# Expert weights in transfers of 2 MB, in the places of the attention's tiles, and gate's last steps behind the gather

## The chip, the cores and the metric

The kernel runs on one core of a Trainium2 chip. The metric is device time of one execution, in microseconds: the median of three timed runs. Profiles are of one execution, which has its own time.

## What is computed

The whole network of three blocks, on 256 tokens of width 1024 in float32. The first block is attention (a windowed unit with grouped heads, and a latent unit) and a mixture of 16 experts. The second is an S5 mixer and a feed-forward block, the third a "fox" attention and a feed-forward block; both are modulated by shift, scale and gate vectors from `silu(c) @ ada_w`. A final norm ends it. The part that the change touches most:

```python
def expert_choice_ffn(h, w_router, w_gate, w_up, w_down):
    cap = CAPACITY_FACTOR * seq // N_EXPERTS      # 2 * 256 // 16 = 32
    aff = softmax(einsum('bsd,de->bse', h, w_router))
    gate, idx = lax.top_k(aff.transpose(0, 2, 1), cap)
    xe = vmap(lambda hb, ib: hb[ib])(h, idx)
    a = silu(einsum('becd,edf->becf', xe, w_gate)) * einsum('becd,edf->becf', xe, w_up)
    ye = einsum('becf,efd->becd', a, w_down) * gate[..., None]
    y = zeros((seq, d)).at[idx].add(ye)           # for each batch
```

Each of w_gate, w_up and w_down is 16 x 1024 x 1024 in float32; together they are 192 tiles of 1 MB, and each is used once.

## The kernel before

Weights come from HBM in the order of one list (`plan` appends to it). `fill` issues the next loads of the list on SP's queue as long as there is a slot; SP then waits, in order, until each slot's last reader is done. A slot is 8 KB in each of the 128 partitions (128x2048 floats, 1 MB), and the pool `big` has 22 of them (NSLOT). Weights share it with the attention's tiles (xT, cn, cT, rev, qk, bqk, qTbv, pT, bqT) and later ones. `weights(room, look, hires, cap)` sets how many slots `fill` leaves free in a stage; `KN` holds these numbers by stage. `done` gives a slot back and calls `fill`.

The experts go in four groups g of four. In a group, for each half hf of the inner width, eight steps k multiply a tile of w_gate and a tile of w_up (four experts side by side on the PE array, into PSUM tiles `pg` and `pu`); after that 16 tiles of w_down give `py`, two halves of eight, each followed by a scatter (`scat`) that adds to h through a one-hot matrix. Tables of the S5 mixer (the `filler`) are computed among the products from the end of the second group on.

Ahead of the experts stands the route (`moe_route`): the affinities' transposes `affT`, eight top-8 steps on DVE, `bi` (indices spread on a diagonal) and the matmul `pidx` that gives them to all partitions, one-hot matrices `oh`, and the gather, eight steps of two matmuls `xe`, interleaved with the first group's first half. Between top-8 and `bi`, `pump(8)` works off the last gate matmuls of the side list: `gate_step` multiplies a piece of `ada_w` with silu(c), and at its last piece copies the sum (`gr`), transposes it, adds a bias (`gc`), transposes again and writes it as a row to DRAM (`row_out`); `fetch` reads it back, near the end of the experts.

Ada loads are eight pieces of 1 MB of `ada_w` for each norm; `ada` are their matmuls, which stand wherever the list of loads brings them. The S5 mixer has four groups n: `u(n)` (a product with a w_in tile), `S` (the chunk's states), a scan with `re`/`im` transposes, `y` and `glu`. `s5m` is the number of loads at the end of the experts' list that stand behind S5's first w_in load.

## Time and profile before

| | us |
|---|---|
| median of three timed runs (1296.58 to 1298.2) | 1297.32 |
| the profiled execution | 1299.42 |
| span of its trace | 1297.1 |
| PE busy | 1109.0 (85%) |
| DVE busy | 658.7 (51%) |
| ACT busy | 401.4 (31%) |
| POOL busy | 107.0 (8%) |

DMA moves 379.35 MB, 292 GB/s in the mean. PE, DVE, ACT and POOL are the four engines, SP the one that issues most DMAs. In the rows below a timeline's line gives start, duration, engine, line of the code, operation, tiles (out<-in), shapes, count, and in brackets the idle time before it with what ended it. The mean granted clock of PE was 0.909.

### The profile page before, as it was taken

The numbers are of one execution on the slowest core, as the hardware profiler recorded it, in microseconds if no ns is written. First come the engines' busy times: TensorE is split into PE (matmuls) and PEld (weight loads), VectorE is DVE, ScalarE is ACT, GpSimd is POOL, SyncE is SP. The second block draws the span as 40 slices with busy tenths as digits, with TensorE's granted clock in tenths as the row PEclk, the third lists the DMA queues.
The fourth block names the chain that finished last, engine by engine and source line by source line (L and its number), as shares of the span: only waits on it lengthen the run. The fifth ranks groups of instructions, "written<-read, shape, count | busy, mean of one in ns | idle before, by whom it ended". The sixth has DMA issues, their size and how long they took to land.

```text
span 1297.1 us, 19439 instructions
## 1 busy us (share of the span) xinstructions
PE 1109.0 (85%) x7775; PEld 747.0 (58%) x7775; DVE 658.7 (51%) x1523; ACT 401.4 (31%) x841; POOL 107.0 (8%) x117
## 2 busy tenths in 40 slices
PE   8989898566666776665989999999999989999997
PEld 7654431011021511100757889998879776999986
DVE  5663401028079507002467666764557765667652
ACT  6352110000000100001014274643444652655541
POOL 2111000010000000000131300000010013200001
PEclk9999897767787867676989999999999989999999
DMA  8994699999999999999775544639665765437420
GB/s 336 389 416 153 260 367 419 418 420 419 420 420 419 418 420 418 420 419 419 308 295 194 194 172 171 247 144 360 209 234 190 289 252 223 142 141 271 153 108 33
DMA packets 61382, 379.35 MB, mean 292 GB/s; under 512 B 6723, under 2 KB 8499, under 8 KB 19692
## 3 DMA queue, kind: packets, MB, share of 16 engines
q1 hardware_dynamic: 60364, 374.49, 73.0%
q0 software_dynamic: 496, 3.23, 0.6%
q8 instruction: 61, 1.00, 0.3%
q10 hardware_dynamic: 432, 0.40, 0.1%
q14 instruction: 29, 0.24, 0.0%
HBM read 376.96 MB, written 1.13 MB: 291 GB/s over the span
## 4 chain that ended last, share of the span: by engine, by line
PE 57%; DMA 29%; DVE 7%; issue 4%; ACT 1%; POOL 1%; SPq 0%; POOLq 0%; DVEq 0%; ACTq 0%
PE up L359 20%; DMA w<-in_w_down_dram 11%; PE acc L359 11%; DMA w<-in_w_up_dram 9%; DMA w<-in_w_gate_dram 6%; PE qk L359 3%; PE wo L359 2%; PE glu L359 2%; PE v L359 2%; DMA row<-row_dram 2%; PE zl L359 1%; PE zq L359 1%; PE xe L359 1%; PE po L359 1%; PE ada L359 1%
## 5 line engine op out<-in xcount | busy, mean ns | idle before, releaser
L291 DVE TENSOR_TENSOR wlo<-w,whi 128x512 fp32r<-128x512 f32 (+4 forms) x284 | 215.8, 821 | 50.3 <-ACT whi L291 46.1
L291 ACT CAST whi<-w 128x512 fp32r<-128x512 f32 (+4 forms) x304 | 191.6, 705 | 69.8 <-PE acc L359 25.8
L359 PE MATMUL up<-xTh,whi 128*128 128x256 f32 x704 | 199.9, 285 | 0.9 <-ACT whi L291 0.9
L359 PE MATMUL up<-xTl,whi 128*128 128x256 f32 x704 | 199.3, 284 | 0.2 <-DVE xTl L400 0.2
L359 PE MATMUL up<-xTh,wlo 128*128 128x256 f32 x704 | 198.8, 283 | 0.0
L359 PEld LDWEIGHTS up<-xTh,whi 128*128 128x128 f32 x704 | 135.4, 193 | 4.9 <-ACT cv L1690 1.7
L359 PEld LDWEIGHTS up<-xTl,whi 128*128 128x128 f32 x704 | 135.3, 192 | 0.6 <-DVE xTl L400 0.6
L359 PE MATMUL py<-w,aT 128*32 128x512 f32 x512 | 91.7, 806 | 51.2 <-DMA w<-in_w_down_dram 51.1
L359 PEld LDWEIGHTS up<-xTh,wlo 128*128 128x128 f32 x704 | 135.1, 192 | 0.2 <-DVE wlo L291 0.2
L359 PE MATMUL pg<-w,xe 128*32 128x512 f32 x512 | 87.6, 761 | 33.4 <-DMA w<-in_w_gate_dram 33.4
L359 PE MATMUL pu<-w,xe 128*32 128x512 f32 x512 | 85.8, 744 | 34.5 <-DMA w<-in_w_up_dram 34.5
L359 PEld LDWEIGHTS py<-w,aT 128*32 128x32 f32 x512 | 12.2, 124 | 119.0 <-DMA w<-in_w_down_dram 102.4
L359 PE MATMUL acc<-whi,gTh 128*128 128x512 f32 (+1 forms) x220 | 76.5, 348 | 0.0
L359 PE MATMUL acc<-whi,gTl 128*128 128x512 f32 (+1 forms) x220 | 76.4, 347 | 0.0
L359 PE MATMUL acc<-wlo,gTh 128*128 128x512 f32 (+1 forms) x220 | 76.2, 347 | 0.0
L402 DVE SCALAR_TENSOR_TENSOR yl<-py,gcol,yh 128x512 fp32r<-128x512 f32 x8 | 6.0, 751 | 127.0 <-ACT yh L401 127.0
L359 PEld LDWEIGHTS pu<-w,xe 128*32 128x32 f32 x512 | 13.9, 120 | 93.3 <-DMA w<-in_w_up_dram 79.0
L359 PEld LDWEIGHTS pg<-w,xe 128*32 128x32 f32 x512 | 13.0, 120 | 89.0 <-DMA w<-in_w_gate_dram 76.4
L1222 DVE TENSOR_TENSOR a<-pu,a 128x512 f32<-128x512 f32 x8 | 5.5, 691 | 107.3 <-PE pu L359 107.3
L401 ACT ACTIVATE yh<-py,gcol 128x512 fp32r<-128x512 f32 x8 | 5.5, 687 | 152.9 <-PE py L359 152.9
L1691 DVE SCALAR_TENSOR_TENSOR cv<-up,small,cv 128x255 f32<-128x255 f32 x44 | 20.9, 482 | 52.9 <-ACT cv L1690 52.7
L1221 ACT ACTIVATE a<-pg 128x512 f32<-128x512 f32 x8 | 4.8, 597 | 136.6 <-PE pg L359 136.6
(451 smaller groups left out, 2001.7 us busy)
## 6 DMA issues: line engine op xcount, KB each, us to landing
w<-in_w_gate_dram SPq DMA_DIRECT2D x64, 1024.0 KB, 19.9
w<-in_w_up_dram SPq DMA_DIRECT2D x64, 1024.0 KB, 19.9
w<-in_w_down_dram SPq DMA_DIRECT2D x64, 1024.0 KB, 19.9
w<-in_ada_t_dram SPq DMA_DIRECT2D x48, 1024.0 KB, 11.3
w<-in_ffn_w_up_dram SPq DMA_DIRECT2D x44, 1024.0 KB, 5.5
w<-in_ffn_w_down_dram SPq DMA_DIRECT2D x22, 1024.0 KB, 7.5
w<-in_fox_w_in_dram SPq DMA_DIRECT2D x12, 1024.0 KB, 5.5
row<-row_dram SPq DMA_DIRECT2D x24, 256.0 KB, 6.8
```

The lines of the kernel that those rows point to most:

```text
L291: for ins in (hc(hi[:, f], t[:, f]), e.tensor_tensor(lo[:, f], t[:, f], hi[:, f].bitcast(F32), op=OP.subtract)):
L359: r = self.nc.tensor.matmul(out, lhsT, rhs, start=start, stop=stop)
L401: return (nc.scalar.mul(dst.hi, src, a), nc.vector.scalar_tensor_tensor(dst.lo, src, a, dst.hi.bitcast(F32), op0=OP.mult, op1=OP.subtract))
L402: nc.vector.scalar_tensor_tensor(dst.lo, src, a, dst.hi.bitcast(F32), op0=OP.mult, op1=OP.subtract))
L1221: nc.scalar.activation(a, pg, AF.Silu)
L1222: nc.vector.tensor_tensor(a, pu, a, op=OP.mult)
L1691: v.scalar_tensor_tensor(cv[:, 1:], a[:, :T - 1], cw[1], cv[:, 1:], op0=OP.mult, op1=OP.add)
```

## The change

Two expert tiles become one transfer. On the host `w_gu` lays w_gate and w_up of a step side by side, `w_dn` two steps of w_down; such a double is 128x4096, 16 KB in each partition, 2 MB. Only the first group's odd steps stay single (`ones`): 24 transfers of 1 MB and 84 of 2 MB in place of 192 of 1 MB.

The slots are split. `big` keeps 14 single ones. Two pools at either side, "l" and "r", have four single slots each, which hold the attention's tiles (xT, rev and bqk left; xt, cn, cT, qk, qTbv, pT and bqT right); when these tiles have been read for the last time, `place` turns each pool into two double ones, and after the experts into four single ones again. So there are at most four doubles at a time. `free` takes tiles, not a count, and `can` asks the pool that a load would go to.

In the route, `held` keeps gate's last steps (`gate_end`) until behind the gather, `one` is made ahead of the top-8 steps, and gather and first half are held in program order. Two numbers of the order change: `s5m` from 4 to 2 (still 4 MB), and `w_moe1`.

```diff
@@ -24,6 +24,8 @@
 NSLOT = 22
+TWOS = 2
-      "sd_firstf": "", "L1": 6, "foxL": 2, "hip": 1, "rm1": -1, "w_moe1": [2, 1, 6],
+      "sd_firstf": "", "L1": 6, "foxL": 2, "hip": 1, "rm1": -1, "w_moe1": [0, 1, 0],
...
-      "s5m": 4, "sd_fox": "a11 g10", "w_ffn01": [7, 2, 2],
+      "s5m": 2, "sd_fox": "a11 g10", "w_ffn01": [7, 2, 2],
+def ones(g, name, hf, k):
+    return (g == 0 or g == 1 and name == "gu" and hf < 0) and k % 2 > 0
-    for name in ("w_gate", "w_up", "w_down"):
-        o[name] = i[name].reshape(4, 4, 8, 128, 2, 512).transpose(0, 4, 2, 3, 1, 5)
+    w = {name: i[name].reshape(4, 4, 8, 128, 2, 512).transpose(0, 4, 2, 3, 1, 5) for name in ("w_gate", "w_up", "w_down")}
+    o["w_gu"] = np.stack([w["w_gate"], w["w_up"]], 4)
+    o["w_dn"] = w["w_down"].reshape(4, 2, 4, 2, 128, 4, 512).transpose(0, 1, 2, 4, 3, 5, 6)
@@ -182,13 +195,42 @@
         self.n += 1
         return f"{s}_{self.n}"
 
-    def slot(self, s, shape=(128, 2048), dtype=F32):
-        assert self.used < NSLOT, f"no slot for {s} (weights {self.wused})"
-        self.used += 1
-        return self.big.tile(list(shape), dtype, name=self.nm(s), tag="s")
-
-    def free(self, k=1):
-        self.used -= k
+    def place(self, x, kind):
+        n = TWOS * (1 if kind == "two" else 2)
+        if x in self.sd:
+            old, cm, _ = self.sd[x]
+            assert self.left[x] == TWOS * (1 if old == "two" else 2)
+            cm.__exit__(None, None, None)
+        more = dict(reuse_waits="tile") if x in self.sd else {}
+        cm = self.tc.tile_pool(name=kind + x, bufs=n, side=dict(l="left", r="right")[x], **more)
+        self.sd[x] = kind, cm, (self.ctx.enter_context(cm) if kind == "late" else cm.__enter__())
+        self.left[x] = n
+    def home(self, k, side=None):
+        want = "two" if k == 2 else "late" if side is None else "one"
+        c = [x for x in (side or "lr") if x in self.sd and self.sd[x][0] == want and self.left[x]]
+        if c:
+            return max(c, key=lambda x: self.left[x])
+        return "big" if k == 1 and side is None and self.left["big"] else None
+    def slot(self, s, shape=(128, 2048), dtype=F32, side=None):
+        k = -(-int(np.prod(shape[1:])) // 2048)
+        x = self.home(k, side)
+        assert x, f"no slot for {s} (weights {self.wused})"
+        self.left[x] -= 1
+        self.used += k
+        t = (self.big if x == "big" else self.sd[x][2]).tile(list(shape), dtype, name=self.nm(s), tag="s")
+        self.at[id(t)] = t, x, k
+        return t
+    def free(self, *tiles):
+        for x in tiles:
+            for t in (x.hi, x.lo) if isinstance(x, Pair) else (x,):
+                _, x, k = self.at.pop(id(t))
+                self.left[x] += 1
+                self.used -= k
 
     def m2k(self, s, shape=(128, 512), dtype=F32):
         return self.mid.tile(list(shape), dtype, name=self.nm(s), tag="m")
@@ -256,11 +298,21 @@
                 self.loads.append(b.pop(0))
         self.loads += a + b
 
+    def can(self, k):
+        if k == 2:
+            return self.home(2) is not None
+        free = self.left["big"] + sum(self.left[x] for x in "lr" if self.sd[x][0] == "late")
+        return free > self.room + max(0, self.hires - self.his) and self.wused < self.cap
     def fill(self, n=1000):
-        while self.pos < min(n, len(self.loads)) and self.used + self.room + max(0, self.hires - self.his) < NSLOT and self.wused < self.cap:
+        while self.pos < min(n, len(self.loads)):
             key, src, shape, split = self.loads[self.pos]
+            k = -(-int(np.prod(shape[1:])) // 2048)
+            if not self.can(k):
+                break
             t = self.slot("w", shape)
-            self.wused += 1
+            self.wused += k
             if callable(src):
                 src(t)
             else:
@@ -643,8 +695,13 @@
             for q in range(4):
                 self.behind_(self.gateps[32 * q:32 * q + 32, :256], self.sc[:, n:n + 1].to_broadcast([128, 32]),
                         t[:, kk, q * 256:(q + 1) * 256], n == 0, n == 7)
-        if k < 3:
-            return
+        if k == 3 and self.held is not None:
+            self.held.append(lambda: self.gate_end(l, b))
+        elif k == 3:
+            self.gate_end(l, b)
+
+    def gate_end(self, l, b):
+        nc = self.nc
         row = self.m2k("gr")
         nc.scalar.copy(row[:, :256], self.gateps[:, :256])
         pc = self.ps("gc")
-                self.free(2)
+                self.free(bq, bk)
-                self.free(2)
+                self.free(*self.rev)
+                self.place("l", "two")
...
-        self.free(4)
+        self.free(both, *bqT, pTt)
+        self.place("r", "two")
@@ -1086,11 +1146,18 @@
-                    for name in ("w_gate", "w_up"):
-                        self.plan(("moe", g, name, hf, k), i[name][g, hf, k], (128, 4, 512), False)
+                    if ones(g, "gu", hf, k):
+                        for n in range(2):
+                            self.plan(("moe", g, "gu", hf, k, n), i["w_gu"][g, hf, k][:, n], (128, 4, 512), False)
+                    else:
+                        self.plan(("moe", g, "gu", hf, k), i["w_gu"][g, hf, k], (128, 2, 4, 512), False)
-                for k in range(8):
-                    self.plan(("moe", g, "w_down", hf, k), i["w_down"][g, hf, k], (128, 4, 512), False)
+                for k in range(4):
+                    if ones(g, "dn", hf, k):
+                        for n in range(2):
+                            self.plan(("moe", g, "dn", hf, k, n), i["w_dn"][g, hf, k][:, n], (128, 4, 512), False)
+                    else:
+                        self.plan(("moe", g, "dn", hf, k), i["w_dn"][g, hf, k], (128, 2, 4, 512), False)
@@ -1147,14 +1216,14 @@
             v.max_index(out=iu[:, o], in_max=top[:, 0, o], in_values=wk)
             wk = nx
         v.tensor_copy(top[:, 1], iu)
+        self.held = []
         self.pump(8)
+        held, self.held = self.held, None
 
         eye = self.ident[:16, :16, None].to_broadcast([16, 16, 32])
         bi = self.m2k("bi", [16, 16, 32], F32R)
         v.tensor_tensor(bi, top[:, 1, None, :].to_broadcast([16, 16, 32]), eye, op=OP.mult)
         pi = self.ps("pidx")
-        one = self.m2k("one", [16, 128], F32R)
-        v.tensor_copy(one, self.ones[:16].to_broadcast([16, 128]))
         self.mm(pi, one, bi.rearrange("e a s -> e (a s)"), True, True)
 
         oh = [self.m2k("oh") for _ in range(2)]
@@ -1181,7 +1250,9 @@
-                self.free()
+                self.free(self.early)
+                for f in held:
+                    f()
@@ -1206,15 +1277,21 @@
             for hf in range(2):
                 pg, pu = self.ps("pg"), self.ps("pu")
                 for k in range(8):
-                    for name, b in (("w_gate", pg), ("w_up", pu)):
-                        key = ("moe", g, name, hf, k)
-                        if name == "w_gate" and g + hf == 0:
-                            next(gather, None)
-                        w = self.get(key)
+                    key = ("moe", g, "gu", hf, k)
+                    one = ones(g, "gu", hf, k)
+                    if g + hf == 0:
+                        next(gather, None)
+                    for n, b in enumerate((pg, pu)):
+                        w = self.get((*key, n)) if one else self.get(key)[:, n]
                         for e in range(4):
                             s = (4 * g + e) * 32
-                            self.mm(b[32 * e:32 * e + 32, :], self.xe[k // 4][:, k % 4, s:s + 32], w[:, e], k == 0, k == 7)
-                        self.done(key)
+                            r = self.mm(b[32 * e:32 * e + 32, :], self.xe[k // 4][:, k % 4, s:s + 32], w[:, e], k == 0, k == 7)
+                            if g + hf == 0:
+                                self.tc.keep_in_program_order(r)
+                        if one:
+                            self.done((*key, n))
+                        elif n:
+                            self.done(key)
                         if g >= 2 or (g == 1 and hf):
                             next(filler, None)
                 a = self.m2k("a", [128, 512])
@@ -1230,18 +1307,24 @@
             if g == 3:
                 for _ in filler:
                     pass
-                self.free(2)
+                self.free(*self.xe)
                 if late:
                     self.weights(*kw("w_moe1", 2, 2, 2))
                     self.fetch(0, 0)
             for hf in range(2):
                 for k in range(8):
-                    key = ("moe", g, "w_down", hf, k)
-                    w = self.get(key)
+                    key = ("moe", g, "dn", hf, k // 2)
+                    one = ones(g, "dn", hf, k // 2)
+                    w = self.get((*key, k % 2)) if one else self.get(key)[:, k % 2]
                     for e in range(4):
                         self.mm(py[hf][32 * e:32 * e + 32, :], aT[k // 4][:, (k % 4) * 128 + 32 * e:(k % 4) * 128 + 32 * e + 32], w[:, e], k == 0, k == 7)
-                    self.done(key)
+                    if one:
+                        self.done((*key, k % 2))
+                    elif k % 2:
+                        self.done(key)
                 self.first("moe_tail" if g == 3 else "", scatter)(g, hf, sc, py[hf])
+        for x in "lr":
+            self.place(x, "late")
 
 
 
```

SP at the end of the experts, before (names are the program's; `w` is a weight's tile, `row` gate's row read back):

```order
L267 DMA w_3414<-in_w_down_dram 128x2048
L267 DMA w_3420<-in_w_down_dram 128x2048
L267 DMA w_3426<-in_s_w_in_dram 128x2048
L267 DMA w_3432<-in_w_down_dram 128x2048
L267 DMA w_3438<-in_w_down_dram 128x2048
L267 DMA w_3444<-in_w_down_dram 128x2048
L267 DMA w_3450<-in_w_down_dram 128x2048
L267 DMA w_3456<-in_s_w_in_dram 128x2048
L267 DMA w_3470<-in_s_w_in_dram 128x2048
L267 DMA w_3472<-in_s_w_in_dram 128x2048
L267 DMA w_3474<-in_ada_t_dram 128x2048
L267 DMA w_3621<-in_ada_t_dram 128x2048
```

and of the change, from S5's second w_in load on (its first stands ahead of the four w_dn of the first half):

```order
L319 DMA w_3258<-in_s_w_in_dram 128x2048
L729 DMA row_3208<-row_dram_89 128x512
L729 DMA row_3209<-row_dram_89 128x512
L729 DMA row_3210<-row_dram_89 128x512
L729 DMA row_3211<-row_dram_89 128x512
L319 DMA w_3224<-in_w_dn_dram 128x4096
L319 DMA w_3234<-in_w_dn_dram 128x4096
L319 DMA w_3246<-in_w_dn_dram 128x4096
L319 DMA w_3256<-in_w_dn_dram 128x4096
L319 DMA w_3324<-in_s_w_in_dram 128x2048
L319 DMA w_3328<-in_ada_t_dram 128x2048
L319 DMA w_3475<-in_ada_t_dram 128x2048
```

S5's second w_in load stood behind the last w_down and now stands ahead of the last four w_dn; each of the last four transfers is a double, and the first ada loads stand behind one w_in load where three stood.

DVE behind the top-8 steps, before:

```order
L1143 MAX early_87<-wk_1299 16x8
L1147 MAX_INDEX early_87<-early_87,wk_1299 16x8
L1149 CAST early_87<-early_87 16x32
L654 TENSOR_TENSOR gc_1341<-gc_1338,small_86 128x8
L1154 TENSOR_TENSOR bi_1350<-early_87,small_86 16x512
L1157 CAST one_1353<-ones_88 16x128
L1162 TENSOR_SCALAR oh_1356<-pidx_1352,early_87,rst_1217 128x512
L1162 TENSOR_SCALAR oh_1357<-pidx_1352,early_87,rst_1217 128x512
```

and of the change:

```order
L1216 MAX_INDEX early_93<-early_93,wk_1303 16x8
L1212 MAX early_93<-wk_1307 16x8
L1216 MAX_INDEX early_93<-early_93,wk_1307 16x8
L1218 CAST early_93<-early_93 16x32
L1225 TENSOR_TENSOR bi_1342<-early_93,small_92 16x512
L1231 TENSOR_SCALAR oh_1346<-pidx_1344,early_93,rst_1221 128x512
L1231 TENSOR_SCALAR oh_1347<-pidx_1344,early_93,rst_1221 128x512
```

`gc` of gate_end stood between the cast of the indices and `bi`; it is now behind the gather's copies, and `one` ahead of the top-8 steps.

TensorE at the start of S5, before, from its first u on:

```order
L359 MATMUL u_3531<-w_3426,xT_3476 128x256 x4
L359 MATMUL ada_3623<-w_3474,sc_329 32x512 x4
L359 MATMUL u_3531<-w_3426,xT_3476 128x256 x12
L359 MATMUL ada_3623<-w_3621,sc_329 32x512 x4
L359 MATMUL ada_3623<-w_3647,sc_329 32x512 x4
L359 MATMUL S_3552<-S_2040,V_3530 32x256 x8
L359 MATMUL ada_3623<-w_3655,sc_329 32x512 x4
L373 MATMUL re_3550<-small_86,z_3561 128x4x32
L373 MATMUL im_3551<-small_86,z_3561 128x4x32
```

and of the change, the same first group:

```order
L425 MATMUL nT_3345<-small_92,hn_3332 128x128 x4
L425 MATMUL nT_3352<-small_92,hn_3333 128x128 x4
L425 MATMUL nT_3371<-small_92,hn_3358 128x128 x4
L425 MATMUL nT_3378<-small_92,hn_3359 128x128 x4
L411 MATMUL u_3385<-w_3236,xT_3330 128x256 x16
L411 MATMUL ada_3477<-w_3501,sc_325 32x512 x4
L411 MATMUL S_3406<-S_2002,V_3384 32x256 x8
L425 MATMUL re_3404<-small_92,z_3415 128x4x32
L425 MATMUL im_3405<-small_92,z_3415 128x4x32
```

The second group's S of the change, where two u groups end:

```order
L411 MATMUL u_3484<-w_3258,xT_3330 128x256 x5
L411 MATMUL u_3512<-w_3324,xT_3330 128x256 x16
L411 MATMUL ada_3477<-w_3509,sc_325 32x512 x4
L411 MATMUL ada_3477<-w_3657,sc_325 32x512 x4
L411 MATMUL ada_3477<-w_3676,sc_325 32x512 x2
L411 MATMUL S_3535<-S_2047,V_3474 32x256 x8
L411 MATMUL ada_3477<-w_3676,sc_325 32x512 x2
L411 MATMUL ada_3477<-w_3990,sc_325 32x512 x4
L411 MATMUL ada_3477<-w_3992,sc_325 32x512 x4
L425 MATMUL re_3533<-small_92,z_3544 128x4x32
```

Of the ada products, one load in place of three stands between the first u and its S; two loads are now ahead of nT, and five around the second group's S, where none stood.

## Rows read from the trace of the kernel before

**Rows 1.** The page, its slices: GB/s in 40 equal parts of the span.
```profile
GB/s 336 389 416 153 260 367 419 418 420 419 420 420 419 418 420 418 420 419 419 308 295 194 194 172 171 247 144 360 209 234 190 289 252 223 142 141 271 153 108 33
```

**Rows 2.** The page, the chain that ended last: shares by engine.
```profile
PE 57%; DMA 29%; DVE 7%; issue 4%; ACT 1%; POOL 1%; SPq 0%; POOLq 0%; DVEq 0%; ACTq 0%
```

**Rows 3.** Chain of waits, 570 to 640 us: start, us, what.
```profile
589.74 18.06 DMA w<-in_w_down_dram
...
607.84 1.83 PE py L359 x8
```

**Rows 4.** DMA traffic, 450 to 570 us: packets; then packets, MB, share by queue.
```profile
DMA packets 6908, 50.34 MB, mean 420 GB/s; under 512 B 766, under 2 KB 766, under 8 KB 766
...
q1 hardware_dynamic: 6904, 50.29, 101.1%
```

**Rows 5.** DMA traffic, 60 to 90 us.
```profile
DMA packets 2226, 12.49 MB, mean 416 GB/s; under 512 B 191, under 2 KB 191, under 8 KB 1215
...
q1 hardware_dynamic: 2224, 12.46, 101.6%
```

**Rows 6.** Timelines of DVE, PE and SP, and DMA landings, around the route.
```profile
152.40 0.17 DVE L1149 CAST early<-early 16x32 f32<-16x32 uint32 x1
...
153.57 0.67 DVE L1154 TENSOR_TENSOR bi<-early,small 16x512 fp32r<-16x512 f32 x1
...
155.84 5.14 PE L359 MATMUL xe<-oh,h 128*128 128x512 f32 x8 [0.90 <-DVE oh L1162]
...
170.01 1.98 PE L359 MATMUL xe<-oh,h 128*128 128x512 f32 x4
...
172.81 1.04 PE L359 MATMUL pu<-w,xe 128*32 128x512 f32 x8
...
162.09 0.33 SPq L267 DMA_DIRECT2D w<-in_w_gate_dram  x1
...
169.29 0.33 SPq L267 DMA_DIRECT2D w<-in_w_gate_dram  x1
...
w<-in_w_gate_dram SPq DMA_DIRECT2D x2, 1024.0 KB, 4.9
```

**Rows 7.** The page, issues to landing; SP's timeline at 421 us.
```profile
w<-in_w_down_dram SPq DMA_DIRECT2D x64, 1024.0 KB, 19.9
...
421.68 0.33 SPq L267 DMA_DIRECT2D w<-in_w_up_dram  x1
...
430.51 18.69 SPq L267 DMA_DIRECT2D w<-in_w_down_dram  x10
```

**Rows 8.** Timeline of PE in the S5 mixer, 616 to 705 us.
```profile
616.36 3.69 PE L373 MATMUL nT<-small,hn 128*128 128x128 f32 x16 [4.35 <-DVE hn L474]
...
621.71 1.06 PE L359 MATMUL ada<-w,sc 128*32 128x512 f32 x8
...
628.09 1.92 PE L359 MATMUL ada<-w,sc 128*32 128x512 f32 x16
...
648.39 1.07 PE L359 MATMUL S<-S,V 128*32 128x256 f32 x16 [0.38 <-DVE V L1487]
...
650.21 0.33 PE L373 MATMUL re<-small,z 128*128 128x128 f32 x1 [0.75 <-ACT z L1499]
...
690.80 1.06 PE L359 MATMUL ada<-w,sc 128*32 128x512 f32 x8
...
702.76 1.07 PE L359 MATMUL gate<-w,sc 128*32 128x256 f32 x16
```

**Rows 9.** Timeline of SP, DMA landings and chain of waits before 62 us.
```profile
26.57 0.30 SPq L718 DMA_DIRECT2D tb_dram<-tb  x1
...
w<-in_w_qb_dram SPq DMA_DIRECT2D x1, 384.0 KB, 12.0
...
44.70 3.87 PE qb L359 x12
```

100 lines of the change are left out of this document (53 added, 47 removed).

## The prediction

> **What bounds the kernel now.** I began with the slices of the page: from the seventh slice to the nineteenth, some 195 to 616 us, the DMA engines move 418 to 420 GB/s, slice after slice [rows 1]. The chain of waits says that this stretch is the path: 29% of the span is DMA, 57% TensorE [rows 2]. Its last link in the experts is the last w_down, in flight 18.06 us up to 607.80; TensorE starts on it at 607.84 and is done after 1.83 us [rows 3]. So from some 173 us to 608 us the time is that of bytes: the end of the experts moves with the rate of the queue and with what stands in it, hardly with engine work. Before that stretch the time is set by the route and the gather, and behind it mostly by TensorE in the S5 mixer and the two feed-forward blocks.
>
> **The change, part by part.** The sums stand against the profiled execution, 1299.42 us; the median of the timed runs is 1297.32, 2.10 less, and I carry the difference over to it at the end.
>
> *Longer rows.* A packet of the trace is one row of a partition. Between 450 and 570 us only 8 KB rows flow: 6904 packets and 50.29 MB take 101.1% of 16 engines, 120 x 16 x 1.011 = 1941 us of engine time [rows 4]. Between 60 and 90 us almost half of the packets of data are shorter: 2224 packets and 12.46 MB take 101.6%, 488 us [rows 5]. With a price a for each MB and b for each packet, 50.29a + 6904b = 1941 and 12.46a + 2224b = 488; so b is 13.2 ns (1 ns either way, from the rounding of the shares) and a 36.8 us. Packets are then 91 us of the 1941, 4.7%. A transfer of 16 KB rows needs half as many packets for its bytes (its closing semaphore writes halve too), so at best 2.35% goes. But shares over 100% say that packets overlap by 1.1%, so a part of b is hidden already; taking that off whole leaves 1.2%. I take the middle, 1.7%; the lower end is nothing, if long rows are cut up into pieces of 8 KB or less. One load of 1 MB takes 120/50.29 x 1.0486 = 2.50 us, a double 5.00 us, so a double saves 0.085 us. Of the 84 doubles the first six land before the queue is full; 78 x 0.085 = **-6.6 us**, between 0 and 78 x 0.1175 = -9.2 us.
>
> The Trainium skill, "DMA: Bandwidth & Descriptors", section "Why small descriptors are slow", gives an overhead of about 3 cycles for each packet, beside one cycle for 32 bytes. By that 8 KB are 259 cycles of which half of 3 go, 0.58%, and the sum would hold -2.3 us here in place of -6.6. The measured 13 ns are above its 3 cycles of 850 MHz (3.5 ns, an estimate from that page); I keep the measurement.
>
> *gate_end behind the gather, `one` ahead.* On DVE `bi` stands right behind gate's `gc` and starts at 153.57, though its input, the cast, is ready at 152.57 [rows 6]. With `gc` gone from ahead of it, `bi`, `pidx` and the gather start some 1.1 us earlier. What is moved (two copies, three small transposes, a row write on SP) lands in a stretch in which TensorE has to wait for DMA soon after, so it costs nothing; were there no cover, it would be the 1.1 us. More comes from the order in the gather: now the slots of k=2 come free after pu at 172.81 + 1.04 = 173.85 [rows 6]. In the changed order only two of the gather's eight products stand between a k and the next. Eight matmul rows take 5.14 us, four take 1.98, a pg and pu together 1.9: 154.74 + 5.14 + 1.9 + 2 x 3.9 = 169.6 for k=2, and 161.8 for k=0. The first double can thus be issued where SP issues the 21st load now (162.09), and the second about 169.6, with 2 MB each and DMA busy from then on. Now the 23rd load, issued at 169.29, lands 4.9 us later [rows 6] and the 24th 2.5 us behind it, at 176.7; then 24 MB would be there at about 174.7, 5 us after the second double's issue: **-2.0 us**, between 0 and -3.
>
> *Four places for doubles.* Now a load is 19.9 us under way, eight in the queue [rows 7]. With four doubles each waits until the one four before it has been used. The queue runs empty only if a place is given back more than 3 x 5 = 15 us after its double landed, less the 2 to 4 us in which TensorE uses it (16 matmuls, as below). The longest pause of SP now is 421.68 to 430.51, 8.8 us, when S5's tables hold TensorE up [rows 7]; so I cost it at nothing, with some 2 to 4 us of cover.
>
> *The end of the experts.* s5's second w_in load (1 MB) now stands behind the last w_down and then stands ahead of the last four: **+2.5 us**. The last transfer is 2 MB, so 16 matmuls wait for its last byte, not 8. At the pace of now they would take 3.66 us for 1.83 [rows 3], at the pace of the ada rows of the same shape, 1.06 for eight [rows 8], 2.1: +0.3 to +1.83, and I take **+1.5 us**, since TensorE waits for bytes up to there, as now. Then TensorE has two ada loads to do before nT. They are the second and third behind the last w_down, landed 7.5 us after it, and done by 9.5; nT starts 616.36 - 607.80 = 8.56 us after the landing now [rows 3, 8] and would start 10 after it: hidden by half a us, else +1.
>
> *S5's ada products.* Before the first S now stand three ada loads, 1.06 and 1.92 us [rows 8]; then one: -2.0. Before and behind the second group's S stand none now, with TensorE idle for 0.38 and 0.75 us there [rows 8]; then five, 2.5 us on either side: +2.1 and +1.75. In return those at 690.80 (1.06) and gate's at 702.76 (1.07) go from the path [rows 8]: -2.1. Net **-0.3**, between -2 and +2.
>
> *The attention.* With fixed places the second w_qb load is issued behind the write of tb at 26.57 and no longer ahead of it. It would land by 38.6 even if it took 12.0 us as now [rows 9], and its product in the new order stands behind all of zq, where TensorE comes at 44.70 [rows 9]: hidden by 6 us. Past 740 us the same work stands in nearly the same order: nothing.
>
> Sum: -6.6 - 2.0 + 2.5 + 1.5 - 0.3 = -4.9, so 1294.5 us for a profiled execution and **1292.4 us** for the median, 0.38% faster.
>
> **The rivals.**
>
> *Rows of 16 KB run no faster for their bytes.* For it: DMA already shows 101.1% [rows 4], and a ceiling of bytes would look the same. Against it: the 13 ns worked out above. The first term goes, the rest is +1.7: 1299.0 us, within 0.2%. The Trainium skill's page on DMA, section "Rules for kernel authors", asks for 1 MiB or more for each transfer and no more than that; by that rule this rival holds. The trace has transfers of just 1 MB at 419 GB/s [rows 1], and can't tell whether more would help.
>
> *Four doubles don't keep the queue full: slower.* Place: the third and fourth group, where S5's tables stand among the products, in the new order in fewer and longer runs between two loads. Each pause of SP beyond 15 - 4 = 11 us costs as much as it exceeds 11. It turns the sign at 4.9 us lost, and is seen as slower from 7.5 us on. Two pauses of 16 us, twice the longest of now, would cost 10: 1302.4 us. Against it: the pause now is 8.8 us [rows 7], and the tables' work is the same.
>
> *S5 pays for the ada loads in full.* If the five before and behind the second group's S also delay its scan, and the two before nT aren't hidden, the sum loses 3 to 4 us more: about 1296 us, a small gain.
>
> **Chances.** Forecast's mechanism 0.58, no faster rows 0.18, S5 pays 0.12, starved queue 0.12. About 0.2% (2.6 us) is what a measurement of this kernel can tell from no change. The forecast's case gives nearly all of faster; S5 pays lies on the border; no faster rows is mostly the same, at times slower; the starved queue is slower in two of three. Together: faster 0.63, same 0.25, slower 0.12. The range takes in the lower end of the first terms (-9.2 - 3 + 2.5 + 0.3 - 2 = -11.4, 1285.9) and the rival without faster rows, 1299.0: 1286 to 1299.
>
> **What would show it.** Slices of 425 to 428 GB/s between 200 and 600 us and doubles landing 4.9 us apart show the first term right; 419 and 5.0 show it wrong. `bi` right behind the cast, and a gather that starts about 1.1 us earlier, show the second. The landing of the last w_dn should lie near 601.7 (607.8 - 6.6 - 2.0 + 2.5), and TensorE's end on it 3.5 us later. SP pauses in the third group of over 11 us, with slices of DMA below 9, would make the prediction wrong; so would an idle TensorE behind the experts that waits for ada's or w_in's loads, or attention units that start later than now.

## The result, and the profile after

The changed kernel takes 1306.72 us (median of 9 runs, 1305.06 to 1309.65) against 1297.46 for the kernel before (median of 9 beside it): a ratio of 1.0069, with a 95% interval of 1.0053 to 1.0085. It is slower by some 9 us, where 1292.4 was forecast. The profiled execution has a span of 1303.6 us, 6.5 more than the 1297.1 of before.

The part up to the end of the experts came out near the forecast: its last products end 5.3 us earlier, where 4.6 were forecast. The page of the changed kernel: the slices of GB/s, then the chain's shares.

```profile
GB/s 310 414 418 145 278 390 424 426 425 428 414 427 428 424 427 428 424 425 410 258 146 225 243 87 270 213 192 274 245 185 236 167 313 280 92 168 283 127 141 33
...
PE 60%; DMA 26%; DVE 8%; issue 2%; ACT 2%; POOL 1%; SPq 0%; POOLq 0%; DVEq 0%; ACTq 0%
```

Most slices of the experts rose from 418 to 420 GB/s to 424 to 428 [rows 1], and DMA's share of the chain fell from 29% to 26% [rows 2]. Its DMA traffic between 450 and 570 us:

```profile
DMA packets 3582, 51.18 MB, mean 426 GB/s; under 512 B 394, under 2 KB 394, under 8 KB 394
...
q1 hardware_dynamic: 3578, 51.12, 100.4%
```

Half the packets carry 1.7% more bytes in the same 120 us [rows 4]. Ahead of the experts, VectorE's timeline: `bi` now stands right behind the cast and three us earlier than in before [rows 6], two of them because the cast itself comes earlier.

```profile
150.27 0.17 DVE L1218 CAST early<-early 16x32 f32<-16x32 uint32 x1
150.48 0.68 DVE L1225 TENSOR_TENSOR bi<-early,small 16x512 fp32r<-16x512 f32 x1
```

TensorE's timeline from the last experts' products to the first product of the feed-forward block shows where the gain starts to go:

```profile
602.44 1.92 PE L411 MATMUL py<-w,aT 128*32 128x512 f32 x16 [1.37 <-DMA w<-in_w_dn_dram]
...
607.43 1.77 PE L411 MATMUL ada<-w,sc 128*32 128x512 f32 x8 [0.68 <-DMA w<-in_ada_t_dram]
609.92 1.94 PE L411 MATMUL ada<-w,sc 128*32 128x512 f32 x8 [0.72 <-DMA w<-in_ada_t_dram]
611.79 2.82 PE L425 MATMUL nT<-small,hn 128*128 128x128 f32 x12
...
623.58 1.05 PE L411 MATMUL S<-S,V 128*32 128x256 f32 x16
...
641.42 2.34 PE L411 MATMUL ada<-w,sc 128*32 128x512 f32 x18
643.17 0.62 PE L411 MATMUL S<-S,V 128*32 128x256 f32 x4
...
644.88 2.35 PE L411 MATMUL ada<-w,sc 128*32 128x512 f32 x18
647.16 0.33 PE L425 MATMUL re<-small,z 128*128 128x128 f32 x1
...
681.37 7.17 PE L411 MATMUL glu<-y,w 128*128 128x256 f32 x32
689.13 1.99 PE L411 MATMUL glu<-y,w 128*128 128x256 f32 x8 [0.59 <-DVE y L1633]
...
700.07 0.66 PE L425 MATMUL adac<-small,adar 128*128 128x128 f32 x4 [1.03 <-ACT adar L678]
702.01 0.27 PE L425 MATMUL gr<-small,adap 128*16 128x128 f32 x1 [1.28 <-DVE adap L685]
...
740.62 3.64 PE L411 MATMUL gate<-w,sc 128*32 128x256 f32 x58
```

The last py ends at 604.36, 5.3 us earlier than before's 609.67 [rows 3]. `nT` is 4.57 earlier, the second group's S 5.2, its `re` 3.05 [rows 8]. Then the ada and gate products that filled waits of TensorE before [rows 8] are missing, and it waits for y, `adar` and `adap`. The sixteen gate products of 702.76 [rows 8] are not gone: they now stand behind S5, where the kernel before has only these 48:

```profile
741.12 2.80 PE L359 MATMUL gate<-w,sc 128*32 128x256 f32 x48
```

In the change there are 64, the last 58 at 740.62. From the first product of s_w_out to the first up the change has no more idle time than before, but is 2.3 us longer.

For all that follows, one window from the last py to the end tells the sum (length; PE, PEld, DVE, ACT and POOL busy with their counts; clock; DMA's share and GB/s). In the kernel before:

```profile
609.67:1297.10 687.43, 654.82 (x5074) 573.89 (x5074) 422.49 (x800) 306.85 (x604) 71.85 (x60) 0.98 0.55 208
```

In the changed kernel:

```profile
604.36:1303.60 699.24, 660.07 (x5075) 575.22 (x5074) 420.52 (x801) 307.07 (x604) 70.80 (x60) 0.98 0.54 204
```

The same work (the matmul count differs by one) takes 11.8 us longer: 6.6 us more with TensorE idle (39.2 against 32.6), and 5.2 us more busy. The clock is only a part of the second: the granted clock is 0.98 in both windows, and by the traces' clock records TensorE is busy for 20.3 us at the lower of its two levels where it was 16.6, which is worth some 1.9 us (an estimate, with products twice as long there, as in s5_loads_moved below). The rest comes with products that stand elsewhere. The gate products in the second feed-forward block's loop of up products, before and after (count; busy us, mean ns; idle time):

```profile
L359 PE MATMUL gate<-w,sc 128*32 128x256 f32 x16 | 1.1, 385 | 0.0
```

```profile
L411 PE MATMUL gate<-w,sc 128*32 128x256 f32 x32 | 3.6, 479 | 0.0
```

Sixteen more stand there, and the loop is 2.2 us longer without more idle time. The first block's loop has the same products in both kernels and is 1.5 us longer; its start, before and after (length, PE busy, clock, DMA's share and GB/s):

```profile
746.00:770.00 24.00, 21.98 (x174) 1.00 0.31 116
```

```profile
746.00:770.00 24.00, 21.97 (x161) 0.93 0.10 39
```

In the same busy time TensorE does 13 fewer products, at a granted clock of 0.93 in place of 1.00.

The largest place past S5 is the norm behind fox. The chain of waits of the changed kernel there:

```profile
1075.49 13.25 DMA row<-row_dram
...
1088.83 1.39 DVE gm L1725 x2
...
1101.32 1.94 PE nT L425 x8
```

The windows of the changed kernel there:

```profile
1090.00:1100.00 10.00, 5.28 (x50) 3.24 (x48) 9.32 (x16) 3.91 (x10) 4.53 (x5) 0.96 0.76 306
1100.00:1110.00 10.00, 8.68 (x57) 6.99 (x58) 3.16 (x5) 3.24 (x6) 5.41 (x5) 0.70 0.00 0
```

And those of the kernel before:

```profile
1090.00:1100.00 10.00, 7.55 (x70) 4.62 (x69) 8.57 (x15) 3.82 (x9) 1.82 (x2) 0.87 0.24 93
1100.00:1110.00 10.00, 10.00 (x82) 10.00 (x82) 1.33 (x3) 3.35 (x6) 5.05 (x4) 0.96 0.09 13
```

The read of the gate's row is on the path for 13.25 us, `gm` and with it the norm wait for it, TensorE is idle for 4.7 us of ten (2.5 in before), and the ten behind them run at a granted clock of 0.70 where it was 0.96. SP issues the six reads of such rows from 1067.23 to 1073.69 in before, one behind the other; in the change six weight loads stand among them, and the last two go out at 1075.49.

The table tells where the time is at eight points: first instruction of each kind on TensorE (for py the end of the last), in us for the kernel before, and for the others how much later (+) or earlier (-). It is read from the timelines; runs of the next section stand beside the change (in_order_most_free is the run loads_in_order_most_free).

| | before | change | short_rows | most_free | oldest_slot | less_weights | s5_loads_moved | in_order_most_free |
|---|---|---|---|---|---|---|---|---|
| last py | 609.6 | -5.3 | +0.5 | -6.1 | -4.8 | -3.6 | +0.2 | -4.0 |
| first glu | 683.7 | -2.3 | +1.2 | -6.0 | -7.3 | -2.2 | -2.2 | -3.9 |
| first product of s_w_out | 717.8 | -2.0 | +1.6 | -0.8 | +2.4 | -1.8 | +12.8 | -3.3 |
| first up, FFN 0 | 746.6 | +0.3 | +4.0 | -0.8 | +2.4 | -1.4 | +13.3 | -3.3 |
| first product of fox's w_out | 1060.0 | +0.8 | +3.5 | -2.4 | +5.0 | -2.3 | +11.9 | -6.9 |
| first nT behind fox | 1092.1 | +4.6 | +7.5 | -2.1 | +7.3 | -2.0 | +11.9 | -6.1 |
| first up, FFN 1 | 1098.8 | +4.2 | +7.1 | -1.6 | +6.4 | -2.0 | +11.7 | -4.7 |
| end | 1297.1 | +6.5 | +8.9 | -0.8 | +7.2 | -2.3 | +12.0 | -5.1 |

Each column is one execution. That of short_rows is the shortest of its seven (1308.1, median 1313.7), that of in_order_most_free the longest of its six (1293.83, median 1290.28), so an end can stand some us from the median. The last py stands between 3.7 and 7.3 us ahead of before in the thirteen profiles with the change's front unaltered; a difference of a us between two columns there says little.

### The profile page after: what moved, and what is told of

Its sections match the earlier page's. It is cut to its first block, busy times and chain, and to the rows that moved or that the text cites. A ratio compares the mean times of both kernels' runs of the same rounds, so it can differ in the third digit from the quotient of the medians.

```text
span 1303.6 us, 19217 instructions
## 1 busy us (share of the span) xinstructions
PE 1093.1 (84%) x7775; PEld 757.9 (58%) x7775; DVE 653.4 (50%) x1523; ACT 401.4 (31%) x841; POOL 108.2 (8%) x117
## 4 chain that ended last, share of the span: by engine, by line
PE 60%; DMA 26%; DVE 8%; issue 2%; ACT 2%; POOL 1%; SPq 0%; POOLq 0%; DVEq 0%; ACTq 0%
PE up L411 20%; DMA w<-in_w_gu_dram 11%; DMA w<-in_w_dn_dram 11%; PE acc L411 9%; PE qk L411 3%; PE pg L411 2%; PE wo L411 2%; PE u L411 2%; PE pu L411 2%; PE ada L411 2%; PE v L411 2%; PE py L411 2%; DMA row<-row_dram 2%; PE glu L411 1%; PE zl L411 1%
## 5 line engine op out<-in xcount | busy, mean ns | idle before, releaser
L411 PE MATMUL py<-w,aT 128*32 128x512 f32 x512 | 79.9, 765 | 58.3 <-DMA w<-in_w_dn_dram 58.3
L411 PEld LDWEIGHTS py<-w,aT 128*32 128x32 f32 x512 | 17.5, 128 | 113.3 <-issue 64.5
L411 PEld LDWEIGHTS pu<-w,xe 128*32 128x32 f32 x512 | 19.7, 129 | 46.1 <-issue 46.1
```

Source lines behind the costliest of these rows:

```text
L411: r = self.nc.tensor.matmul(out, lhsT, rhs, start=start, stop=stop)
```

## The experiments

The first theory: behind the experts the 22 slots are three pools (14, 4 and 4) and `home` hands out the four-slot pools first, so loads, ada and gate products and row reads come in another order. By the order of names in the two traces, 24 of the last 160 DMAs that SP issues stand elsewhere than in before, and some 690 of the 5074 matmuls behind the experts. The rivals: being early is worth nothing there; or the front's other edits are to blame.

**Which slot, and the front's edits.** The first run lets a single tile take the pool with the most free slots, by two lines in `home`; the second returns "big" in their place, the big pool first:

```diff
+        if k == 1 and side is None and self.left["big"]:
+            c.append("big")
```

> The changed kernel, but behind the experts a single load goes to whichever of the three pools (14 big, 4 left, 4 right) has most free slots, not to left and right first. Theory 'pools' (the time behind the experts is lost because the loads there wait for a slot of their own small pool, so ada, gate and row loads and their products move): the experts still end about 5 us earlier than before, and the time behind them goes back by most of the 12 us lost there, total 1290 to 1296. Theory 'shift' (the order behind the experts changes because they end earlier, whatever the pools): no gain against the change, 1303 to 1308. Theory 'front' (the experts themselves are slower in runs without a profile): 1303 to 1308 too, with a trace that ends early.

Measured: 1299.68 us, ratio 1.0022 (1.0011 to 1.0032). Seven of the nine us come back, short of the theory's 1290 to 1296; in its profile 5.2 us go between the first glu and s_w_out.

> The same, with the big pool always first and left and right only when it is full. Pools: as the run before, 1290 to 1297, with gate's products again in the hole ahead of nT. Shift and front: 1303 to 1308.

Measured: 1307.53 us, 1.0087 (1.0067 to 1.0107). No gain, where the theory had 1290 to 1297: glu pieces slip in among y, and 10 us go there. So it isn't enough to avoid the small pools; it points to the order that comes out.

The third makes all 192 transfers 1 MB again and keeps only the pools (`ones` returns True; each side becomes four single slots as soon as the attention leaves it; the two numbers of the planner for it are those of before):

> The changed kernel with all 192 expert transfers of 1 MB (8 KB a partition); the left and right pools are turned into four single slots each at once, and the two numbers of the order are those of before. Pools: it loses behind the experts as the change does, and lacks its faster rows, so it is the slowest, 1305 to 1312; slices at 418 to 420 GB/s. If the 2 MB transfers themselves were the loss: 1294 to 1298.

Measured: 1336.36 us, 1.0309 (1.0287 to 1.0331), far above the 1305 to 1312 expected; the last py is 20.6 us late, behind it another 15 are lost. The page of its slices:

```profile
GB/s 308 413 408 141 322 414 420 419 406 375 420 420 417 398 420 419 420 408 377 116 346 129 176 62 316 146 196 331 243 148 282 132 282 329 64 190 251 133 154 32
```

Slices dip to 375 and 398, but that is little beside 20 us. Ahead of the experts' last load SP issues seven more other loads of 1 MB than in before (five of ada, one of s_w_in, one of s_w_out); at 2.5 us for 1 MB [rows 4] that is some 17 us of the queue, an estimate, and most of the delay. So the run shows how far pools can move the order, and is no test of 2 MB against 1 MB.

The fourth puts gate's last steps ahead of `bi` again (`held = []` in place of `self.held = []`):

> The changed kernel with gate's last steps again ahead of bi (one still ahead of the top-8 steps, gather and first half still in program order). Pools: 1 us or less slower than the change, bi about 1 us later, nothing else moves, 1305 to 1309. If holding gate's steps were the loss: 1296 to 1300.

Measured: 1306.12 us, 1.0075 (1.0051 to 1.0099). The gather starts 1.7 us later, the last py ends 0.5 later, the end is the same: that edit is neither the loss nor much of the gain.

**The slot freed first.** `home` keeps the time at which each free slot was given back, and takes the oldest, as one pool would:

```diff
+            c += ["big"] if self.left["big"] else []
+            return min(c, key=lambda x: self.since[x][0]) if c else None
```

> The change with one rule altered: a tile of one slot that names no side goes to the pool whose free slot was freed first, as the one pool of before gives its slots out. Theory (the loss behind the experts is the order in which the three pools let loads, and with them the ada and gate products and the row reads, come): TensorE's products from S5's end on stand as before, so most of the 12 us that the change loses behind the experts comes back, and the experts' end stays some 5 us early: 1293 to 1298 us. It keeps what the most-free rule lost inside glu (about 5 us, the scan of the last groups) if that is set by VectorE and not by slots. Rival (being early in S5 is worth nothing whatever the slots' order, since VectorE's scan sets S5's end): the start of the first up product as before, 1297 us and no better. Second rival (the order is no cause): 1306.

Measured: 1308.14 us, 1.0084 (1.0060 to 1.0108). The theory in this form fell: the end is 12 us later than the last py would make it, though only some 250 of TensorE's matmuls are moved, where the change moves 690. The first glu is 7.3 us early and s_w_out 2.4 late: TensorE does 32 glu products ahead of the scan's end, waits 1.75 and 1.52 us for y, and 2.57 for `adar`, whose copy stands behind two casts on ScalarE.

> The rule of oldest_slot up to the end of S5, the change's own rule (late pools first) from the first FFN on. If the loss is two losses, one around S5 (about 5.5 us between the experts' end and the first up product) and one in fox and the second FFN (about 6 us, row reads behind weight loads), this gives back the first alone: about 1300 to 1302 us, and the wait of nT behind fox for VectorE's hn stays near 6 us. Rival (what is held at the end of S5 decides the later order too): as oldest_slot, within 1.5 us.

> The change's own rule up to the end of S5, the rule of oldest_slot from the first FFN on. Two losses: the first up product starts as in the change (746.9), the loss in fox and the second FFN comes back, about 1300 to 1302 us. Rival (the later order follows from what S5 leaves): as the change, 1306.

Measured: 1307.11 (1.0086, 1.0058 to 1.0115) and 1302.65 us (1.0032, 1.0017 to 1.0047). The split did not do what was written: the mark of the stage on which the rule looked is cleared by the stage's first product, so the first of the two is almost oldest_slot and the second almost the change, with another rule for a few loads at each stage's start. They don't split the loss. But the second shows that a few loads can move 4 us.

**The row's length alone.** The weights are laid out so that a 2 MB transfer reads two rows of 8 KB; all queues are those of the change:

```diff
-    o["w_gu"] = np.stack([w["w_gate"], w["w_up"]], 4)
+    o["w_gu"] = np.stack([w["w_gate"], w["w_up"]], 3)
-                        self.plan(("moe", g, "gu", hf, k), i["w_gu"][g, hf, k], (128, 2, 4, 512), False)
+                        self.plan(("moe", g, "gu", hf, k), i["w_gu"][g, hf, k].rearrange("n p e f -> p n e f"), (128, 2, 4, 512), False)
...
```

> The change with the experts' weights laid out so that a transfer of 2 MB reads two rows of 8 KB a partition and not one of 16 KB; tiles, pools, transfers and the order of the products are those of the change. Theory (the front's gain of 5.3 us is the row's length in DRAM, 13 ns a packet, and early routing's 3): slices of 418 to 420 GB/s, the experts' end about 4 us later than in the change, near 608.5 us, and the time some 2 to 4 us above the change's, 1308 to 1310, if S5 passes it on. Rival (the gain is fewer transfers or the larger tiles): slices stay at 424 to 428 GB/s and the time at the change's 1306.

Measured: 1313.7 us, 1.0126 (1.0103 to 1.0150), 7 us above the change and above the 1308 to 1310 expected. Its slices, and the last experts' products in its chain of waits:

```profile
GB/s 307 405 416 157 286 389 420 418 420 421 420 419 420 419 420 420 420 418 414 254 190 197 259 89 279 205 191 274 251 170 251 164 306 288 86 173 289 117 144 33
```

```profile
606.84 3.28 PE py L411 x16
```

418 to 421 GB/s again, with transfers of 2 MB. TensorE starts on the last transfer at 606.84 where the change starts at 602.44, though the gather began 0.8 us earlier: from the gather's first product to there 455.0 us against 449.8. The last py ends 5.7 us later than in the change, 1.3 of them since these products take longer here. The front's gain is the row.

**Early, with the queues left alone.** The kernel before with two loads fewer; it also leaves out the eight products that use them, so its sums lack that step:

```diff
-                for k in range(8):
+                for k in range(8 - (g == 0 and hf == 1)):
```

> The kernel before, with its one pool, without two of its 192 transfers of experts' weights (gate's and up's last row block of the first group's second half, 2.1 MB, about 4.9 us at 428 GB/s; their eight products are left out of the sums). Its S5 then starts as early as the change's, and behind the experts every queue is left nearly as it was. Theory (what the change loses behind the experts is the other order of its queues, not that it comes early): the 5 us pass through to the end, 1292 to 1293 us. Rival (coming early is worth nothing, since VectorE's scan or TensorE's clock sets S5's end): 1296 to 1298, as before.

Measured: 1294.9 us, 0.9972 (0.9956 to 0.9989). The last py comes 3.6 us earlier (the route came 1.2 us later in this profile), the end 2.3: two thirds pass. Behind the experts some 60 of TensorE's matmuls stand elsewhere, of SP's DMAs none. By the medians it gains 4.0 us, where 2 MB take some 5 us of the queue. The rival that being early is worth nothing falls.

**S5's end put back by hand.** oldest_slot with glu's first eight products bound between the y of the third and the fourth group, and these y kept in program order:

```diff
...
+        for n in range(1):
+            glu_a(n)
         outputs(3)
...
```

> oldest_slot with S5's end put back near the order of before: glu's first eight products stand between the y of the third and of the fourth group by program order, and not among the y ahead of the fourth group's rotation. oldest_slot lost 9.7 us between the first glu product and the first product of s_w_out, with glu waiting 1.8 and 1.5 us for VectorE's y, 2.6 for the ada row, at half clock around it. Theory (the order of TensorE's queue there is the loss): most of it comes back, the first product of s_w_out comes 4 to 6 us earlier than in before, and the end 1291 to 1295 us, under before. Rival (the fourth group's scan on VectorE holds S5's end whatever stands in TensorE's queue): 1297 to 1302. A second rival: fox's own order takes 4 us or more behind it again, 1297 to 1299.

Measured: 1302.86 us, 1.0035 (1.0022 to 1.0048), not under before as the theory had it. Its part on S5 holds: s_w_out's first product and the first up come 5.5 us earlier than in before. The second rival holds too, and not in fox alone: 5.1 us go in the first loop of up products, another 5 around fox. TensorE's waits between 741 and 883 us (for what; us in total, times, longest):

```profile
PE up L420 <- ACT whi L352: 2.3, 1, 2.3
PE gc L434 <- ACT gr L715: 1.8, 1, 1.8
```

SP's queue had a weight load behind a row write that waited 26.4 us, so the next two runs issue row writes from ScalarE's queue (`self.nc.scalar.dma_start` for `self.nc.sync.dma_start` in `row_out`).

> oldest_slot_glu_placed with the write of a gate's row to DRAM issued from ScalarE's queue, behind the copy that makes it, and not from SP's, where it waited 26.4 us for that copy with the loads of the FFN's weights behind it. TensorE's order is unchanged. There the loop of up products was 5.1 us longer than in before, with TensorE waiting 2.3 us for a cast whose weight had been queued behind that write (759.91). Theory (a load's place behind a waiting row is what the change costs there): the loop is back at 137 us, the start of its first product stays near 741, and the end comes 4 to 6 us earlier, 1296 to 1299 us, under or at before; less still if fox's loads were held in the same way. Rival (the loop lost by the gate clock after the idle in the norm alone): 1302 to 1303.

Measured: 1302.89 us, 1.0049 (1.0030 to 1.0068): no gain. All three up loads are now issued at 732.78 and TensorE still waits 2.3 and 1.8 us. ScalarE's timeline says why:

```profile
752.21 2.18 ACT L352 CAST whi<-w 128x512 fp32r<-128x512 f32 x4 [0.75 <-PE up L420]
754.41 1.28 ACT L1800 ACT_TABLE_LOAD   x1
...
756.48 0.36 ACT L715 COPY gr<-gate 128x256 f32<-128x256 f32 x1
```

Four casts for a later weight stand ahead of the table load, so the copy for `gc` is late, and then the casts that `up` needs. By this trace the order of ScalarE's queue costs here, not a load's place.

> The change with that one edit (row writes issued from ScalarE's queue); TensorE's order is the change's. Theory (row writes that wait at the head of SP's queue, 43 us in five waits against 61 in six in before, hold back loads whose place the three pools moved): the stretch from the first up product to the end, 6.2 us longer than in before, gets 2 to 4 of it back, 1302.5 to 1304.5 us. S5's loss stays. Rival (SP's queue has slack there, and the loss is TensorE's and VectorE's order alone): 1306 to 1307.

Measured: 1305.19 us, 1.0064 (1.0046 to 1.0083). That is 1.5 us under the change, between the theory and the rival, and the two intervals overlap almost wholly: if row writes on SP's queue are a part of the loss, it is a small one.

**Loads in the order of the plan.** Behind the experts each weight load is bound to be issued behind the one planned before it, with the rule of the most free pool. The binding was not run on the kernel before.

```diff
-                self.nc.sync.dma_start(t, src)
+                r = self.nc.sync.dma_start(t, src)
+                if key[0] == "s5_w_glu" or "load" in self.after:
+                    self.line_up(r)
+    def line_up(self, r):
+        x = self.after.get("load")
+        if x is not None:
+            self.tc.add_manual_dep(r.ins, x.name, ...)
+        self.after["load"] = r.ins
```

> most_free with each weight load behind the experts bound to be issued behind the load planned before it; 8 of 160 DMAs of SP then stand elsewhere than in before, and TensorE's products at S5's end (y, glu with four ada products between, y, glu) stand as in before but for six y. Theory (order of loads, and through it of the products): the 5.2 us that most_free lost between the first glu product and the first of s_w_out come back, and the end is 1293 to 1296 us, under before. Rival (slots of the wrong pool, not the order, hold things up): as most_free or later, 1299 to 1303, with SP waiting longer at the head of its queue.

Measured: **1290.28 us, 0.9938 (0.9922 to 0.9955)**, the first whole version under both kernels. TensorE's timeline at S5's end has the order of before [rows 8], four us earlier:

```profile
679.85 7.17 PE L422 MATMUL glu<-y,w 128*128 128x256 f32 x32
686.95 1.06 PE L422 MATMUL ada<-w,sc 128*32 128x512 f32 x8
687.95 2.42 PE L422 MATMUL glu<-y,w 128*128 128x256 f32 x10
...
692.84 5.31 PE L422 MATMUL glu<-y,w 128*128 128x256 f32 x22
699.18 0.66 PE L436 MATMUL adac<-small,adar 128*128 128x128 f32 x4 [1.03 <-ACT adar L689]
699.77 1.07 PE L422 MATMUL gate<-w,sc 128*32 128x256 f32 x16
```

glu and ada fill the wait for the fourth group's scan, gate the wait for `adap`. The 4.0 us at the last py are 5.1 at the end. The pools, `s5m` and `w_moe1` are those of the change, so none of these costs the time by itself. The gate products stand where they stood in before, and no row read is late behind fox.

> oldest_slot with the loads behind the experts in planned order; 5 of SP's 160 DMAs stand elsewhere than in before. TensorE's order in S5's end still has glu products among the y of the third group, as in oldest_slot, so part of its 9.7 us there stays. Theory: 1297 to 1302 us, the up loops and fox as long as in before (137 and 79 us). Rival (order of loads is no cause): 1307 to 1308 as oldest_slot.

Measured: 1303.02 us, 1.0041 (1.0026 to 1.0056). The first up loop is as long as before, but S5's end loses 6.7 us to glu among y, as foretold, and fox 5.2, which was not: loads in order are not enough where casts and products stand elsewhere.

> The change itself with the loads behind the experts in planned order, its slot rule kept: 12 of SP's 160 DMAs stand elsewhere than in before (24 in the change). TensorE's order barely follows (eight ada products still stand ahead of nT, eight and eight around the second group's S, gate's behind acc). Theory (the order of loads matters through TensorE's, ScalarE's and VectorE's queues, which this leaves): 1303 to 1306 us, little of the loss back. Rival (the order of loads matters by their arrival alone): most of it back, 1296 to 1300.

Measured: 1306.89 us, 1.0071 (1.0052 to 1.0090): the change's own rule with loads in planned order gains nothing: TensorE's order barely follows. In its profile 5.8 us go between the last product of fox's w_out and the first nT behind it, at the row reads again. The planned order of loads alone is not it.

**The order alone, in the kernel before.** One pool, rows of 8 KB, no edit but the string that mixes ada's loads (s) among S5's (m):

```diff
-"mx_s5": "ssmssmssmmssmmmm"
+"mx_s5": "ssmsssmsssmmmmmm"
```

> The kernel before, one pool, rows of 8 KB; only the plan that mixes ada's loads among S5's weights is altered to the order that the change's SP queue has (three ada loads to a glu load, the last two glu loads behind them). Behind S5 all queues stay as in before; in S5 four ada products stand ahead of the second group's S, twelve ahead of the fourth group's re, glu's last loads come later. Theory (the order alone costs, without any pool): 2 to 4 us slower than before, 1299.5 to 1301.5 us, all of it between the experts' end and the first product of s_w_out. Rival (the pools cost, the order does not): 1297 to 1298, as before.

Measured: 1309.44 us, 1.0083 (1.0062 to 1.0104). The order alone costs 12 us, more than the whole change loses, and three times the upper end of what I expected. TensorE's timeline there:

```profile
681.48 2.26 PE L359 MATMUL glu<-y,w 128*128 128x256 f32 x6
...
684.03 1.99 PE L359 MATMUL glu<-y,w 128*128 128x256 f32 x8
...
688.71 0.70 PE L359 MATMUL glu<-y,w 128*128 128x256 f32 x2
696.32 3.78 PE L359 MATMUL glu<-y,w 128*128 128x256 f32 x8 [6.92 <-DVE y L1550]
...
704.17 1.99 PE L359 MATMUL glu<-y,w 128*128 128x256 f32 x8 [1.52 <-DVE y L1550]
...
707.58 0.66 PE L373 MATMUL adac<-small,adar 128*128 128x128 f32 x4 [1.42 <-ACT adar L626]
```

Its window from 690 to 700 us:

```profile
690.00:700.00 10.00, 3.68 (x8) 2.52 (x8) 6.27 (x21) 0.00 (x0) 3.16 (x3) 0.66 0.56 200
```

With two of glu's loads behind the last ada loads, TensorE has nothing left while VectorE scans the fourth group: it waits 6.92 us, and the eight glu products behind that take 3.78 us, 0.47 each, where thirty-two take 7.17, 0.22 each, in the run above: the lower of the clock's two levels. 96 glu products are left for later, where before 64 were.

**What the best version gains by.** The same order with rows of 8 KB, and with row writes off SP's queue:

> loads_in_order_most_free with two rows of 8 KB a partition to each transfer of 2 MB, as in short_rows; all queues as in loads_in_order_most_free. Theory (the row's length is the front's gain and nothing takes it back in this order): the experts' end 5 to 6 us later and the time with it, 1295 to 1297 us, at before's. Rival (the gain against before is S5's order, not the rows): 1290 to 1292.

Measured: 1298.60 us, 1.0007 (0.9995 to 1.0020): no different from before. In this order TensorE starts on the last transfer at 601.94 us with long rows and at 607.31 with short ones, and the medians differ by 8 us (the two profiles by 3.6): within the noise the row's length is the whole gain.

> loads_in_order_most_free with the gates' rows written from ScalarE's queue; TensorE's order unchanged. Theory (a row write that waits holds the loads behind it): 0.5 to 2 us earlier, 1288.5 to 1290 us, as the 1.5 us in the change. Rival (those loads have slack in this order): 1290.3, within what the measurement tells.

Measured: 1291.02 us, 0.9944 (0.9931 to 0.9957): the same as without the edit. The rival holds: in this order the row writes on SP's queue cost nothing that can be told.

## Why the prediction was wrong

*The bound and the rows: right.* The rate rose by what was worked out from the packets. From the gather's first product to TensorE's start on the last transfer the change takes 449.8 us and short_rows 455.0; loads_in_order_most_free takes 449.1 and in_order_short_rows 454.9. So the rows give 5.2 to 5.9 us for the forecast 6.6.

*Gather, `one`, gate and the second w_in: right in sum.* -2.0 and +2.5 were to leave +0.5 at the start on the last transfer with rows as before; short_rows, with the change's route and old rows, starts 1.0 us ahead of before there (606.84 against 607.84 [rows 3]). From the cast to the gather it is 2.40 us where it was 3.44, as forecast. That the gather began 3.2 us earlier and not 1.1 came from the attention, which had been put at nothing: it ends at 141.1 to 142.3 us in the three profiles with before's front and at 138.4 to 141.4 in the others. Some half of that reached the experts' end, a gain that the sum did not count.

*The last double: too dear.* +1.5 was forecast; 16 products took 1.92 us where eight took 1.83 [rows 3], so +0.1. That was luck: by the traces' clock records the clock was at its upper level there, and at its lower one at the last py of before. In the four runs of these 16 products at the lower level (oldest_slot, short_rows, loads_in_order_most_free and in_order_short_rows) they take 3.2 to 3.6 us, as the +1.5 had it.

*Four doubles: right.* SP's longest wait for py was 11.7 us, over the 11 that I had called the limit, and no slice of the experts fell below 410 GB/s.

*ada ahead of nT: the cover of half a us was not there.* The two loads were waited for (0.68 and 0.72 us), and nT stands 4.57 us earlier where the last py is 5.25 earlier: +0.7.

*S5's ada products, -0.3: failed.* The gain before the first S came (another 1.7 us), and five ada loads around the second group's S cost 3.2 of the 3.85 us. But the -2.1 for the ada and gate products that go from 690.80 and 702.76 did not: these had filled waits, not caused them. In their places TensorE waits 0.59, 1.03 and 1.28 us, and between the first glu and s_w_out 0.3 us are lost where 2.1 should be gained; the gate products come back behind S5 and cost 2.3 us there. s5_loads_moved shows the size of this step when most of the cover goes: 15 us.

*"Past 740 us the same work stands in nearly the same order: nothing": failed, and the largest.* Behind the nT at 740 the change loses 7.7 us (from 1.2 us ahead to 6.5 behind). By stages: 1.5 us up to the first up (the moved gate products), 1.5 in the first up loop (the clock), 3.9 from fox's w_out to the norm behind it (the row reads), 2.2 in the second up loop (gate products again); 1.4 come back in small pieces. Two more runs have the change's order on TensorE, short_rows and rows_off_sp: there the first is 1.5 and 1.6, the third 4.0 and 5.0, the fourth 1.7 and 1.7, and the second is missing. I had compared TensorE's order in S5 and looked at what lay behind only by kinds of work; SP's 24 moved DMAs and the casts behind them I did not weigh. in_order_most_free, with 8 of them moved, loses nothing past 740.

*The rivals.* Rows that run no faster and a starved queue fell by the slices of 424 to 428 GB/s. "S5 pays for the ada loads in full" had the right place for the first 4 us and the wrong reason for a part of them; none told of an order that costs to the end. With another slot rule and the loads kept in order the time is 1290.28, near the 1292.4 forecast for the change as it was: what the front gives was sized right to a us or so (in part by the luck of the clock), what lies behind was not.

What stays open: what each move past 740 us would give back if it alone were undone. The gate products, the row reads and the lower clock were each seen at a place, the first two in three runs, but not taken away one at a time in the change; the split that should have told S5 from the rest did not split. That the pools move the order, that an order alone can cost 12 us, and that the same pools with other rules for slots and loads lose nothing, is shown; that every us of the change's loss is order is argued from these places.

## What to carry to other kernels

When slots are split into pools, a load waits for a slot of its own pool, and a scheduler that puts instructions where they are ready can move them, and with them products and casts behind: compare the issue order on every queue up to the last instruction, not only around the edit, and bind the loads to the old order where it served. Work that fills a wait is cover: before counting its removal as a gain, look at what the engine would wait for in its place, and at where the work will stand instead, since there it may cost its full time. In these runs a front that came earlier passed on what it gained where the queues behind it stayed nearly as they were (two thirds in less_weights), and not where they moved.

## What the runs showed of the hardware that was not expected

A transfer of 2 MB to 128 partitions runs at 424 to 428 GB/s with one row of 16 KB a partition and at 418 to 421 with two of 8 KB, in a kernel that is otherwise the same: 449.8 against 455.0 us from the gather to the last transfer, 449.1 against 454.9 in the order that passes it on, and there 0.7% of the whole time (0.9938 against 1.0007). And an idle stretch can cost twice: in s5_loads_moved 6.92 us of waiting for y were followed by matmuls at 0.47 us each in place of 0.22, with a granted clock of 0.66 in the ten us around them.
